# Adding the down-projection results to the residual rows by accumulating DMAs instead of on VectorE, in a decoder layer on one Trainium2 core

## The chip, the cores and the metric

The kernel runs on one core of a Trainium2 chip. The metric is the device time of one execution in microseconds (us); several runs are made, and their median is quoted. Engines are named as in the profile: PE is TensorE's matmuls, PEld its weight loads, DVE is VectorE, ACT is ScalarE, POOL is GpSimd, and SP is SyncE, which issues most DMAs. All arithmetic is on 32-bit floats.

## The reference, cut to what matters

One decoder layer over 256 rows of width 2048. The change touches the first and the last sub-layer, the two feed-forward networks (width 5632), with the DeepNorm residual around each:

```
x = layer_norm(ALPHA * x + 0.5 * (silu(x @ w_gate) * (x @ w_up)) @ w_down, ln1_g, ln1_b)
... attention sub-layer: x = layer_norm(ALPHA * x + mix, ln2_g, ln2_b) ...
x = layer_norm(ALPHA * x + 0.5 * (silu(x @ w_gate) * (x @ w_up)) @ w_down, ln3_g, ln3_b)
```

The kernel computes twice the argument of the feed-forward norms, `2*ALPHA*x + ffn(x)`, and makes up for the factor in the norm's epsilon.

## The kernel before, in words

**Rows and residual.** The 256 rows are two row tiles `t` of 128 partitions. `y[t]` (128x2048 f32, in SBUF) holds the residual rows; column block `n` is 512 wide. In the first network `y` is the input, loaded in eight pieces by `load_y` from SP's queue, one after each weight piece of the first up product. In the second network it is the normalised output of attention: `ln_res` multiplies by the gain (L591) and adds the bias (L592) on DVE, with gain and bias loaded by POOL's queue (L587, L588).

**Products.** Each f32 product is made of three matmuls of rounded halves: `split` writes `hi` on ACT (L91) and the remainder `lo` on DVE (L92), and `mm3` issues hi*hi, lo*hi and hi*lo (L96 to L98). Weights come by DMA into `raw` tiles, are split into `whi` and `wlo` tiles (six of each), and only then can PE use them.

**`gemm2`** makes a 256x1024 product (two row tiles, two column blocks) from weight pieces of 256 rows. For some pieces (`seven`) it uses seven block products for eight: DVE makes sums of weight blocks (L293 to L295), which are split as well, and the seven products gather in PSUM banks. After the last such piece ACT and DVE combine four banks into four `w` tiles (L332 to L336; `w` has nine buffers). At its end, DVE adds each remaining bank to its `w` tile (L345), and `finish` takes the four results.

**Order.** A network runs: gate 0, up 0, gate 2, up 2, gate 4, **down 0**, up 4, gate 6, up 6, gate 8, **down 1**, up 8, the last columns, down 2. The down product is so cut along its inner dimension into three groups `gi`, and each group adds its result to `y`. Groups 0 and 1 are two `gemm2` each (`cp` 0 and 1), so there are four results of 128x512 at the end of each, and 2 networks x 2 groups x 2 = 8 such ends, at about 262, 303, 513, 554, 1312, 1353, 1564 and 1605 us. In `down`, `fin` adds a result on DVE: for group 0 it also scales (`y = 2*ALPHA*y + result`, L503), for groups 1 and 2 it is a plain add (L505). After group 2 the norm follows.

**Queues.** PE and SP run in the order in which the code is written. On DVE, ACT and POOL a list scheduler sets the order at build time from its own estimates; on the chip each engine then goes strictly in that order.

Of the kernel before, what the change touches and what calls it, by code (L numbers as in the profile page):

```python
# [14 lines left out]
OP = mybir.AluOpType  # L15
# [3 lines left out]
P = 128  # L19
D = 2048  # L20
S = 256
NT = S // P
FF = 5632
KD = D // P
NCH = 512
ALPHA = 2.0 ** 0.25
# [13 lines left out]
GATE, GATE7 = (0, 1, 2, 3, 4, 5, 6, 7), (2, 4, 5)  # L40
UP, UP7 = (0, 1, 3, 2, 4, 6, 5, 7), (1, 2, 4, 5)
# [8 lines left out]
def layer(ctx: ExitStack, tc: tile.TileContext, a: dict, out: bass.AP):  # L50
    nc = tc.nc
    PE, V, A, G = nc.tensor, nc.vector, nc.scalar, nc.gpsimd
# [127 lines left out]
    def new_bank():  # L180
        return bank.tile([P, NCH], F32, name="bank")
# [166 lines left out]
    def new_T():  # L348
        return (tp.tile([P, 4, P], F32R, name="thi"), tp.tile([P, 4, P], F32R, name="tlo"))

    def sl(pair, j):
        return pair[0][:, j, :], pair[1][:, j, :]
# [5 lines left out]
    y = [const.tile([P, D], F32, name=f"y{t}") for t in range(NT)]  # L358
# [12 lines left out]
    def parts(s):  # L371
        hl = am2(F32R)
        split(*hl, s)
        return hl
# [50 lines left out]
    def ffn(name, x, xs, done, begin=None, after=None, late=()):  # L425
        wg, wu, wd = (W[name + n] + (W2[name + n][0],) for n in ("_w_gate", "_w_up", "_w_down"))
        groups = [[0, 1, 2, 3], [4, 5, 6, 7], [8, 9, 10]]
        late = list(late)
        hT, hS, hs, sg = {}, {}, {}, {}

        def trans(cs, ready, want=()):

            for c in cs:
                v, sums_too = [], c in want
                for t in range(NT):
                    while held[0] or now[0] < ready:
                        yield 1
                    pt = new_bank().rearrange("p (a b) -> p a b", a=4)
                    for j in range(4):
                        PE.transpose(pt[:, j, :], hs[c, t][:, j * P:(j + 1) * P], ident)  # L440
                    hT[c, t] = new_T()
                    src = pt
                    if sums_too:
                        src = wk([P, 4, P])
                        A.copy(src, pt)
                        v.append(src)
                    A.copy(hT[c, t][0], pt)
                    V.tensor_tensor(hT[c, t][1], src, f(hT[c, t][0]), op=OP.subtract)  # L448
                    if t and sums_too:
                        for i in range(KT):  # L450
                            hS[2 * c + i] = parts(sums([u[:, KT * i + j] for u in v for j in range(KT)]))
                    yield 1

        def gate(c0):
            def fin(t, j, r):
                A.activation(r, r, AF.Silu)
                sg[c0 + j, t] = r

            if c0:
                gemm2(x, xs, GATE, GATE7, name + "_w_gate", c0 // 2, fin)  # L460
                return
            def first(t, j, ps):
                sg[j, t] = wk([P, NCH])
                A.activation(sg[j, t], ps, AF.Silu)

            def rest(at):
                if begin and at == 7:
                    cst.update(load_consts())
                for _ in range(2):
                    if late:  # L470
                        late.pop(0)()

            gemm2(x, xs, GATE, (), name + "_w_gate", 0, first, each=rest, head=0 if begin else 4, pre=begin)

        def up(c0):
            def fin(t, j, r):
                hs[c0 + j, t] = sg[c0 + j, t]
                V.tensor_tensor(hs[c0 + j, t], r, sg[c0 + j, t], op=OP.mult)

            gemm2(x, xs, LATE if c0 in (4, 8) else UP, UP7, name + "_w_up", c0 // 2, fin, each=after if c0 == 0 else None)  # L480
            spawn(trans((c0, c0 + 1), now[0] + DFF, (0, 1, 4, 5, 9)), "T")

        def last():

            def fin(t, j, r):
                if j == 0:
                    A.activation(r, r, AF.Silu)
                    hs[10, t] = r
                else:
                    V.tensor_tensor(hs[10, t], r, hs[10, t], op=OP.mult)  # L490

            gemm2(x, xs, GATE, GATE7, name + "_gu", 0, fin)
            spawn(trans((10,), now[0] + DLAST), "T")

        def down(gi):
            grp = groups[gi]
            ks = list(range(grp[0] * 4, (grp[-1] + 1) * 4))
            xh = lambda k, t: sl(hT[k // 4, t], k % 4)

            def fin(t, n, ps):  # L500
                yc = y[t][:, n * NCH:(n + 1) * NCH]
                if gi == 0:
                    V.scalar_tensor_tensor(yc, yc, 2 * ALPHA, ps, op0=OP.mult, op1=OP.add)  # L503
                else:
                    V.tensor_tensor(yc, ps, yc, op=OP.add)  # L505
                if gi == 2:
                    done(t, n)

            for cp in range(2):
                if gi < 2 or cp == 0:  # L510
                    base = 2 * grp[0]
                    order, sevens = (DOWN, DOWN7) if gi < 2 else (range(6), (2, 3))
                    gemm2(xh, hS, [base + i for i in order], [base + i for i in sevens], name + "_w_down", cp,
                          lambda t, j, r: fin(t, 2 * cp + j, r))
                    continue
                for n in (2 * cp, 2 * cp + 1):
                    gemm(xh, wd, n, ks, lambda t, ps: fin(t, n, ps), tail=6 if n == 3 else 0)


        for step, n in ((gate, 0), (up, 0), (gate, 2), (up, 2), (gate, 4), (down, 0), (up, 4), (gate, 6), (up, 6), (gate, 8),  # L520
                        (down, 1), (up, 8)):
            step(n)
        last()
        down(2)
# [56 lines left out]
                    xs.setdefault(2 * n + j, []).extend(v[:, 2 * j + i, :] for i in range(2))  # L581
            yield 1

    def ln_res(name, n):

        g, b = wk([P, NCH]), wk([P, NCH])
        G.dma_start(g, bcast(a[name + "_g"][0, n * NCH:(n + 1) * NCH], NCH))  # L587
        G.dma_start(b, bcast(a[name + "_b"][0, n * NCH:(n + 1) * NCH], NCH))  # L588
        for t in range(NT):
            yc = y[t][:, n * NCH:(n + 1) * NCH]  # L590
            V.tensor_tensor(yc, yc, g, op=OP.mult)  # L591
            V.tensor_tensor(yc, yc, b, op=OP.add)  # L592

    def ln_out(t, eps, gb):
        mu, r = ln_rows(t, eps)
# [10 lines left out]
        load_x(max(1, 2 * i), 2 if i else 1)  # L606

    def load_y(i):
        t, n = i // 4, i % 4
        nc.sync.dma_start(y[t][:, n * NCH:(n + 1) * NCH], a["x"][t * P:(t + 1) * P, n * NCH:(n + 1) * NCH])  # L610


    w0, ps0 = wk([P, NCH]), new_bank()
# [470 lines left out]
    def sum2(i):  # L1084
        xs2[i] = parts(sums(xs2[i]))

    ffn("ffn2", lambda k, t: sl(x2[k // 4, t], k % 4), xs2, done3,
        late=[lambda i=i: sum2(i) for i in UP7] + [lambda n=n: ln_res("ln2", n) for n in range(4)])
    drain()


# [74 lines left out]
```

## Time and profile before

| | |
|---|---|
| median of 3 runs (lowest to highest) | 1767.45 us (1766.21 to 1768.01) |
| the profiled execution: its own time, and its span | 1766.0 us, 1764.3 us |
| PE busy | 1745.0 us (99%) |
| DVE busy | 1596.6 us (90%) |
| ACT busy | 997.8 us (57%) |
| POOL busy | 17.4 us (1%) |
| DMA: SP's queue, POOL's queue | 58.1% and 0.8% of 16 engines' span |
| chain that ended last, by engine | PE 74%, DVE 17%, DMA 3%, issue 3%, ACT 2% |

The own time is the device time of that one execution; the span goes from its first to its last instruction. A busy PE here is a PE with a matmul in flight; matmuls overlap, so whether PE is at its pace is read from the distance between their starts.

### The profile page before, as it was taken

To read this page: it belongs to the slowest core of one execution; us is meant where nothing else is said; L and a number is where in the kernel's file an instruction comes from. 1 tells how busy PE (TensorE), PEld (TensorE's weight loads), DVE (VectorE), ACT (ScalarE), POOL (GpSimd) and SP (SyncE) were. 2 spreads that over 40 slices of the span, in tenths; PEclk is the share of its full clock that TensorE was granted. 3 is DMA by queue.
4 is the path that set the end of the run, shared out by engine and by line. 5 is a ranking of instruction groups with operands and counts; after the bars stand their busy time and mean duration, and the time that the engine had idled before them with its cause. 6 is when DMAs were issued, how large, how long until landed. Compare 5 with 4: busy or idle time off the path is not lost.

```text
span 1764.3 us, 22385 instructions
## 1 busy us (share of the span) xinstructions
PE 1745.0 (99%) x8018; PEld 1429.0 (81%) x8018; DVE 1596.6 (90%) x2121; ACT 997.8 (57%) x1324; POOL 17.4 (1%) x40
## 2 busy tenths in 40 slices
PE   9999999999999999999999999999999999999997
PEld 7888888888888888887788778888888888888886
DVE  7899999999999998766576679899999999999997
ACT  6656555575655565654555555565655565655651
POOL 0000000000000000000000001000000000000000
PEclk9999999999999999999999999999999999999999
DMA  9665656556567557546843355656556656566654
GB/s 335 219 209 176 209 200 203 192 189 211 196 197 230 193 177 255 182 143 210 300 153 120 123 176 171 211 179 198 196 193 224 203 185 209 196 196 216 203 197 162
DMA packets 103440, 350.01 MB, mean 198 GB/s; under 512 B 11152, under 2 KB 13728, under 8 KB 103328
## 3 DMA queue, kind: packets, MB, share of 16 engines
q1 hardware_dynamic: 102016, 344.37, 58.1%
q0 software_dynamic: 1312, 4.21, 0.8%
q8 instruction: 63, 1.03, 0.2%
q14 instruction: 49, 0.40, 0.1%
HBM read 346.44 MB, written 2.10 MB: 198 GB/s over the span
## 4 chain that ended last, share of the span: by engine, by line
PE 74%; DVE 17%; DMA 3%; issue 3%; ACT 2%; SPq 0%; POOL 0%; DVEq 0%; ACTq 0%; POOLq 0%
PE bank L97 23%; PE bank L98 23%; PE bank L96 23%; DVE wlo L92 8%; DVE sum L293 2%; DVE w L345 2%; ACT whi L91 1%; DMA raw<-in_ffn_w_down 1%; DVE sum L295 1%; DVE sum L294 1%; DMA raw<-in_ffn_w_up 1%; DVE tlo L448 1%; PE bank L1004 1%; DMA raw<-in_w_in 1%; PE bank L994 1%
## 5 line engine op out<-in xcount | busy, mean ns | idle before, releaser
L96 PE MATMUL bank<-whi,thi 128*128 128x512 f32 (+1 forms) x1958 | 771.9, 394 | 0.0
L97 PE MATMUL bank<-wlo,thi 128*128 128x512 f32 (+1 forms) x1958 | 761.2, 389 | 1.5 <-DVE wlo L92 1.4
L98 PE MATMUL bank<-whi,tlo 128*128 128x512 f32 (+1 forms) x1958 | 761.1, 389 | 0.0
L91 ACT CAST whi<-raw 128x1024 fp32r<-128x1024 f32 (+2 forms) x569 | 533.1, 965 | 264.7 <-PE bank L98 123.2
L92 DVE TENSOR_TENSOR wlo<-raw,whi 128x1024 fp32r<-128x1024 f32 (+2 forms) x569 | 624.0, 1111 | 63.6 <-ACT whi L91 62.9
L91 ACT CAST whi<-sum 128x1024 fp32r<-128x1024 f32 x267 | 279.2, 1050 | 369.3 <-DVE sum L295 143.2
L96 PEld LDWEIGHTS bank<-whi,thi 128*128 128x128 f32 x1958 | 368.0, 188 | 79.1 <-issue 5.4
L98 PEld LDWEIGHTS bank<-whi,tlo 128*128 128x128 f32 x1958 | 367.6, 188 | 76.5
L97 PEld LDWEIGHTS bank<-wlo,thi 128*128 128x128 f32 x1958 | 368.2, 188 | 75.8 <-DVE wlo L92 3.8
L92 DVE TENSOR_TENSOR wlo<-sum,whi 128x1024 fp32r<-128x1024 f32 x267 | 319.3, 1214 | 26.0 <-ACT whi L91 23.7
L97 PE MATMUL bank<-wlo,m 128*128 128x512 f32 x424 | 166.0, 392 | 2.0 <-DVE wlo L92 2.0
L96 PE MATMUL bank<-whi,m 128*128 128x512 f32 x424 | 165.1, 389 | 0.0
L98 PE MATMUL bank<-whi,m 128*128 128x512 f32 x424 | 165.1, 389 | 0.0
L293 DVE TENSOR_TENSOR sum<-raw 128x1024 f32<-128x1024 f32 x106 | 129.0, 1217 | 9.1 <-DMA raw<-in_ffn_w_down 5.0
L97 PEld LDWEIGHTS bank<-wlo,m 128*128 128x128 f32 x424 | 79.5, 188 | 22.3 <-DVE wlo L92 5.5
L96 PEld LDWEIGHTS bank<-whi,m 128*128 128x128 f32 x424 | 79.6, 188 | 16.6
L98 PEld LDWEIGHTS bank<-whi,m 128*128 128x128 f32 x424 | 79.6, 188 | 16.0
L345 DVE TENSOR_TENSOR w<-bank,w 128x512 f32<-128x512 f32 x120 | 78.7, 681 | 0.2
L295 DVE TENSOR_TENSOR sum<-sum,raw 128x512 f32<-128x512 f32 x106 | 72.3, 683 | 0.2
L294 DVE TENSOR_TENSOR sum<-sum,raw 128x512 f32<-128x512 f32 x106 | 72.3, 683 | 0.0
L733 ACT ACTIVATE w<-w,mx 128x256 f32<-128x256 f32 (+1 forms) x48 | 21.4, 446 | 29.8 <-DVE mx L729 28.1
L440 PEld LDWEIGHTS bank<-ident,w 128*128 128x128 f32 x176 | 21.9, 140 | 5.8
(190 smaller groups left out, 889.7 us busy)
## 6 DMA issues: line engine op xcount, KB each, us to landing
raw<-in_ffn_w_down SPq DMA_DIRECT2D x169, 512.0 KB, 4.7
raw<-in_ffn_w_up SPq DMA_DIRECT2D x160, 512.0 KB, 4.8
raw<-in_ffn_w_gate SPq DMA_DIRECT2D x146, 512.0 KB, 5.0
raw<-in_ffn_gu SPq DMA_DIRECT2D x32, 512.0 KB, 4.2
raw<-in_w_in SPq DMA_DIRECT2D x30, 512.0 KB, 5.1
raw<-in_w_out SPq DMA_DIRECT2D x20, 512.0 KB, 3.3
sum<-in_w_in SPq DMA_DIRECT2D x18, 512.0 KB, 5.4
sum<-in_ffn_w_gate SPq DMA_DIRECT2D x12, 512.0 KB, 4.1
```

Of the source, the lines that this page charges most:

```text
L91: A.copy(hi, src)
L92: V.tensor_tensor(lo, src, f(hi), op=OP.subtract)
L96: PE.matmul(ps, xh, wh, start=first, stop=False)
L97: PE.matmul(ps, xh, wl, start=False, stop=False)
L98: PE.matmul(ps, xl, wh, start=False, stop=last)
L293: V.tensor_tensor(t13, a_, b_[:, 1:2, :].broadcast_to([P, 2, NCH]), op=OP.add)
L294: V.tensor_tensor(t24[:, 0], t13[:, 0], a_[:, 1], op=OP.add)
L295: V.tensor_tensor(t24[:, 1], t24[:, 0], b_[:, 0], op=OP.add)
L345: V.tensor_tensor(rest[b], B[b], rest[b], op=OP.add)
L440: PE.transpose(pt[:, j, :], hs[c, t][:, j * P:(j + 1) * P], ident)
L448: V.tensor_tensor(hT[c, t][1], src, f(hT[c, t][0]), op=OP.subtract)
L733: A.activation(s[:, h, :], s[:, h, :], AF.Exp, bias=mx[:, h:h + 1], accum_out=sm[:, h:h + 1])
```

## The change

For groups 0 and 1 the four results of each `gemm2` are no longer added by DVE but by DMAs issued from POOL's queue that add their source to the destination in SBUF. As such a DMA only adds, `y` is multiplied by `2*ALPHA` beforehand, on ACT: in the first network two weight pieces after the load of each piece of `y` (the last two during gate 2), in the second network at the end of `ln_res`. Group 2 is left as it was.

```
-                gemm2(x, xs, GATE, GATE7, name + "_w_gate", c0 // 2, fin)
+                gemm2(x, xs, GATE, GATE7, name + "_w_gate", c0 // 2, fin,
+                      each=(lambda i: after(8 + i)) if after and c0 == 2 else None)
...
             def fin(t, n, ps):
                 yc = y[t][:, n * NCH:(n + 1) * NCH]
-                if gi == 0:
-                    V.scalar_tensor_tensor(yc, yc, 2 * ALPHA, ps, op0=OP.mult, op1=OP.add)
+                if gi < 2:
+                    G.dma_start(yc, ps, accum_op=OP.add)
                 else:
                     V.tensor_tensor(yc, ps, yc, op=OP.add)
-                if gi == 2:
                     done(t, n)
...
+    def scale_y(t, n):
+        yc = y[t][:, n * NCH:(n + 1) * NCH]
+        A.mul(yc, yc, 2 * ALPHA)
+
-    def ln_res(name, n):
+    def ln_res(name, n, scale=False):
...
             V.tensor_tensor(yc, yc, b, op=OP.add)
+            if scale:
+                scale_y(t, n)
...
     def load_y(i):
-        t, n = i // 4, i % 4
-        nc.sync.dma_start(y[t][:, n * NCH:(n + 1) * NCH], a["x"][t * P:(t + 1) * P, n * NCH:(n + 1) * NCH])
+
+        if i < 4 * NT:
+            t, n = i // 4, i % 4
+            nc.sync.dma_start(y[t][:, n * NCH:(n + 1) * NCH], a["x"][t * P:(t + 1) * P, n * NCH:(n + 1) * NCH])
+        if 0 <= i - 2 < 4 * NT:
+            scale_y((i - 2) // 4, (i - 2) % 4)
...
-        late=[lambda i=i: sum2(i) for i in UP7] + [lambda n=n: ln_res("ln2", n) for n in range(4)])
+        late=[lambda i=i: sum2(i) for i in UP7] + [lambda n=n: ln_res("ln2", n, True) for n in range(4)])
```

DVE's instructions at the end of the first network's first down `gemm2` (about 262 us; `y_92` and `y_93` are `y` of the two row tiles), before:

```order
L294 TENSOR_TENSOR sum<-sum,raw 128x512
L92 TENSOR_TENSOR wlo<-raw,whi 128x512
L345 TENSOR_TENSOR w<-bank,w 128x512 x2
L503 SCALAR_TENSOR_TENSOR y_92<-y_92,w 128x512
L345 TENSOR_TENSOR w<-bank,w 128x512
L503 SCALAR_TENSOR_TENSOR y_93<-y_93,w 128x512
L503 SCALAR_TENSOR_TENSOR y_92<-y_92,w 128x512
L345 TENSOR_TENSOR w<-bank,w 128x512
L295 TENSOR_TENSOR sum<-sum,raw 128x512
L503 SCALAR_TENSOR_TENSOR y_93<-y_93,w 128x512
L92 TENSOR_TENSOR wlo<-sum,whi 128x1024 x2
```

The same place in the change:

```order
L294 TENSOR_TENSOR sum<-sum,raw 128x512
L92 TENSOR_TENSOR wlo<-raw,whi 128x512
L345 TENSOR_TENSOR w<-bank,w 128x512 x4
L295 TENSOR_TENSOR sum<-sum,raw 128x512
L92 TENSOR_TENSOR wlo<-sum,whi 128x1024
```

The four L503 are gone, and the block sum L295 with the splits behind it moves up by that much. The other seven ends read alike (L505 for L503 in group 1).

ACT's instructions near the end of the first network's first up product (75 to 84 us), before:

```order
L91 CAST whi<-sum 128x1024 x2
L91 CAST whi<-raw 128x1024 x2
L332 COPY w<-bank 128x512
L91 CAST whi<-raw 128x1024 x5
L91 CAST whi<-raw 128x512
```

The same place in the change (L586 is `scale_y`):

```order
L91 CAST whi<-sum 128x1024
L586 ACTIVATE y_93<-y_93 128x512
L91 CAST whi<-sum 128x1024
L91 CAST whi<-raw 128x1024 x2
L332 COPY w<-bank 128x512
L91 CAST whi<-raw 128x1024 x5
```

The scaling of the last piece of `y` now stands between two weight splits; the first seven stand in the same manner ahead of it, one or more splits apart. POOL's queue gets 16 adding DMAs in a row per network, and nothing stands between them.

## Rows read from the trace of the kernel before

**Rows 1.** Windows: busy us of PE, PEld, DVE, ACT, POOL; clock, DMA share, GB/s.

```profile
300.00:350.00 50.00, 50.00 (x222) 41.40 (x221) 49.32 (x60) 25.83 (x29) 0.00 (x0) 1.00 0.59 199
...
1550.00:1600.00 50.00, 49.42 (x217) 40.18 (x216) 48.61 (x57) 27.05 (x30) 0.00 (x0) 1.00 0.63 205
```

**Rows 2.** Timeline of PE: start us, us, engine, line, operation, near 300 us.

```profile
299.69 0.39 PE L96 MATMUL bank<-whi,thi 128*128 128x512 f32 x1
...
301.96 0.39 PE L97 MATMUL bank<-wlo,thi 128*128 128x512 f32 x1
```

**Rows 3.** Waits of PE over the span, longest first: us in total, times, longest.

```profile
PE bank L97 <- DVE wlo L92: 3.4, 9, 0.7
```

**Rows 4.** Timeline of PE at four waits: in brackets idle and releaser.

```profile
393.42 0.39 PE L96 MATMUL bank<-whi,thi 128*128 128x512 f32 x1
394.28 0.50 PE L97 MATMUL bank<-wlo,thi 128*128 128x512 f32 x1 [0.47 <-DVE wlo L92]
...
394.85 0.40 PE L96 MATMUL bank<-whi,m 128*128 128x512 f32 x1
395.42 0.50 PE L97 MATMUL bank<-wlo,m 128*128 128x512 f32 x1 [0.17 <-DVE wlo L92]
...
1323.44 0.39 PE L96 MATMUL bank<-whi,m 128*128 128x512 f32 x1
1324.09 0.50 PE L97 MATMUL bank<-wlo,m 128*128 128x512 f32 x1 [0.26 <-DVE wlo L92]
...
1575.21 0.40 PE L96 MATMUL bank<-whi,m 128*128 128x512 f32 x1
1576.19 0.50 PE L97 MATMUL bank<-wlo,m 128*128 128x512 f32 x1 [0.58 <-DVE wlo L92]
```

**Rows 5.** Chain by line: 292 to 396, 1290 to 1326, 1540 to 1577 us.

```profile
by line: DVE wlo L92 33.9%; issue 13.1%; DMA raw<-in_ffn_w_up 10.0%; DVE sum L293 8.9%; DVE w L345 5.9%; DVE sum L295 4.7%; DVE sum L294 4.7%; ACT whi L91 4.0%; DVE m L92 2.0%; DVE y L503 1.9%; DVE w L478 1.9%; DVE tlo L448 1.7%; DVE w L333
...
by line: DVE wlo L92 36.6%; DMA raw<-in_ffn_w_down 17.7%; DVE sum L293 9.9%; issue 9.3%; DVE y L503 6.7%; DVE w L345 6.7%; DVE sum L294 5.0%; DVE sum L295 5.0%; PE bank L97 2.7%; PE bank L98 1.9%; PE bank L96 1.3%; DVEq L293 0.1%
...
by line: DVE wlo L92 38.7%; DMA raw<-in_ffn_w_down 18.9%; DVE sum L293 9.5%; DVE sum L295 6.7%; DVE w L345 6.5%; DVE y L505 6.5%; issue 6.5%; DVE sum L294 4.9%; PE bank L97 1.3%; PE bank L96 0.6%; PE bank L98 0.6%; DVEq L293 0.1%
```

**Rows 6.** Groups by form: line, engine, operation, shapes, xcount; busy us, mean ns; idle before.

```profile
L505 DVE TENSOR_TENSOR y<-w,y 128x512 f32<-128x512 f32 x24 | 16.0, 678 | 0.0
...
L503 DVE SCALAR_TENSOR_TENSOR y<-y,w 128x512 f32<-128x512 f32 x16 | 10.6, 682 | 0.0
```

**Rows 7.** Groups by form: the nearest ACT instruction, 128x512 from SBUF to SBUF.

```profile
L456 ACT ACTIVATE w<-w 128x512 f32<-128x512 f32 x32 | 19.4, 633 | 7.0 <-DVE w L345 7.0
```

**Rows 8.** The last load of `y` (SP's queue), and ACT's split at 78 us.

```profile
L610 SPq DMA_DIRECT2D y<-in_x x1: 421/421/421, 73.5 to 73.5; - x1
...
DMA to landing us min/median/max: 4.9/4.9/4.9
...
78.44 1.05 ACT L91 CAST whi<-sum 128x1024 fp32r<-128x1024 f32 x1 [1.89 <-DVE sum L295]
```

**Rows 9.** Window of 1072 to 1090 us, and its DMAs by queue and tile.

```profile
1072.00:1090.00 18.00, 18.00 (x81) 14.92 (x80) 17.99 (x31) 10.85 (x12) 4.32 (x8) 1.00 0.76 264
...
q0 software_dynamic: 640, 2.10, 39.0%
...
raw<-in_ffn_w_up SPq DMA_DIRECT2D x5, 512.0 KB, 6.2
```

**Rows 10.** Page, DMA issues: engine, xcount, KB each, median us to landing.

```profile
raw<-in_ffn_w_up SPq DMA_DIRECT2D x160, 512.0 KB, 4.8
```

**Rows 11.** Timeline of DVE: first add of a result, next reuse of `w`.

```profile
261.97 0.68 DVE L503 SCALAR_TENSOR_TENSOR y<-y,w 128x512 f32<-128x512 f32 x1
...
292.18 0.68 DVE L333 TENSOR_TENSOR w<-bank,w 128x512 f32<-128x512 f32 x1
```

**Rows 12.** Windows behind two ends of down products: columns as in the first group.

```profile
1311.00:1316.00 5.00, 5.00 (x24) 4.14 (x23) 5.00 (x10) 0.00 (x0) 0.00 (x0) 1.00 0.33 108
1316.00:1321.00 5.00, 5.00 (x24) 4.14 (x23) 5.00 (x5) 3.46 (x4) 0.00 (x0) 1.00 0.31 105
```

## The prediction

> **What bounds the kernel now.** I read the windows first, then the timeline of PE, PE's waits, and the chain behind the larger waits. In the feed-forward stretches PE and DVE are full at once: from 300 to 350 us PE is busy 50.00 of 50 us with 222 matmuls, DVE 49.32 [rows 1]. Which of the two sets the pace is read from PE's starts. Near 300 us there are 11 starts from 299.69 to 301.96 us, that is 0.227 us each [rows 2], and 222 matmuls of that length fill 50 us. So PE runs at its own pace there, and a DVE that gets freer does not make it faster. DVE counts only where PE stands still for it. Those places are few: PE waits for the low half of a weight (`wlo`) nine times, 3.4 us in all [rows 3]. From 1550 to 1600 us one sees it: 217 matmuls instead of 222, with DVE at 48.61 [rows 1]. The 17% that DVE holds of the chain of the whole kernel is therefore no measure of the gain; most of it is work that PE's own pace hides, and the reader is to keep the 3.4 us in mind as the size of what can be had.
>
> Four of the nine waits have an add of a down result in the chain behind them. At 1323 us PE's starts are 0.65 us apart where 0.227 is normal, at 1575 us 0.98, at 393 us 0.86 and at 395 us 0.57 [rows 4]. Over the normal distance that is 0.42 + 0.75 + 0.63 + 0.34 = 2.14 us. The chain into the first two is DVE work nearly throughout, and the adds hold 6.7% of 36 us and 6.5% of 37 us of it, 2.4 us each, which are the four adds of one end; in the chain into 393 us L503 holds 1.9% of 104 us, 2.0 us [rows 5]. Each share is larger than the wait at its end.
>
> **What is removed.** 32 adds on DVE: 16 of 0.682 us and 16 of the 24 rows of 0.678 us [rows 6], 21.8 us of DVE, 2.7 us at each of the eight ends of a down `gemm2`. DVE's order shows that the block sum L295 and the splits behind it move up by the four adds. Taken out of the chain, 2.0 to 2.4 us are more than the 0.42, 0.75 and 0.63 + 0.34 us that PE waits, so these four waits should go: 2.14 us. What is late next is PE itself, which then goes on at 0.227 us. At the other ends PE does not wait, so 2.7 us less of DVE buys nothing there; up products and the attention have none of the removed rows. The other five of the nine waits I leave as they are: I found no add in the stretches behind them.
>
> **What is added on ACT.** 16 scalings of 128x512. The trace has no such multiply; the nearest row is an activation of that size from SBUF to SBUF, 0.633 us [rows 7]. That is 10.1 us, hidden by an ACT that is busy 26 to 27 of 50 us [rows 1]. Without that cover it would cost up to 0.63 us each. The order can make it dearer, since ACT goes strictly in turn: a scaling whose piece of `y` has not landed holds up the weight splits behind it, and these hold up DVE and then PE. The worst is the last one. Its load is issued at 73.5 us and lands 4.9 us later, at 78.4; ACT stands idle for 1.89 us up to 78.44, waiting for DVE, just where the order puts the scaling [rows 8]. So the scaling waits for 1.8 us that are idle anyway, and the split behind it starts 0.6 us late. A delay of 0.6 us is a third of the one gap shown, and ACT is idle for nearly half of its time, so I put all 16 at 0; the bound above is eight pieces at 0.6 us, 5 us, if nothing hid them. In the second network the scalings wait for DVE's L592, which comes at its time as before, and stand between splits in the same manner.
>
> **What is added as DMAs.** 32 adds of 256 KB, issued by POOL, which is otherwise idle. The trace has no adding DMA and none within SBUF. The nearest are POOL's loads of the norm's gain and bias, also 128x512. Eight of them fall in 1072 to 1090 us and take 39.0% of 18 us of all 16 DMA engines [rows 9], 0.88 us each. Four adds at that price are 3.5 us per end. I take that as the lower bound, since an add must also read what it adds to.
>
> The Trainium skill has the price of that second read: in "Collectives: The Full Stack" (The bandwidth ceiling) the add itself is free, but two sources are read for each write on one ring, and the measured rate is about half. By it an add would be an estimated 1.8 us and an end 7 us, and the sum would stay, since that is no more than the eight loads took together.
>
> Whether it matters is a question of how late the weights come. The eight loads are a fair rehearsal, 7.0 us of DMA in one burst: the five weight loads in that window land in 6.2 us [rows 9] against 4.8 [rows 10], 1.4 us later, and PE loses nothing (81 matmuls in 18 us, busy 18.00). And the adds come at a good moment: after an end the DMA share is 0.33 and 0.31 for ten microseconds [rows 12], because the raw buffers are held by DVE work. A delay of 1.4 us is less than the 2.4 us by which DVE is now earlier. I take 0, and carry what is left to the second rival.
>
> The adds bring one new wait: a `w` tile may be written again only when its DMA is done. After the first end the next writers are ACT's L332 and DVE's L333; DVE's comes 30 us after the first add [rows 11], ACT's a little before it. So four adds may take some 7 us each before L332 waits, with the weight splits behind it on ACT and PE behind those. Behind an add on POOL stand only other adds until the norm. Group 2 reads `y` only after two more whole products, up 8 and the last columns.
>
> **The sum.** From the profiled execution's 1766.0 us: less 2.14 for the four waits, 0 for ACT, 0 for the DMAs, makes 1763.9. That execution lies 1.45 us under the median of the runs shown, 1767.45, so the median is forecast at 1765.3, 0.12% less. A difference under 0.2%, 3.5 us, I call no change: it is about what a measurement of this kernel can tell.
>
> **The rivals.** *Every wait for DVE goes.* If the earlier DVE carries over into the other five waits too, or they go with a shifted order, the gain is at most all 3.4 us of idleness. Four waits with 1.48 us of idleness cost 2.14 us, 1.45 times as much, so 4.9 us, and the time is 1762.5. For it: DVE is near 50 of 50 us for long stretches, so time saved can travel far. Against it: none of the five has a removed add in the stretch behind it.
>
> *The stalls stay.* DVE may spend what it saves waiting for the high halves, which ACT can only write once PE frees a buffer; then the lead is the same when the next heavy stretch comes, and the changed order can put another sum or split late. Then the time is 1767.4. For it speaks that DVE's order also changed where nothing was removed; against it that the chains into 1323 and 1575 us run without a break of PE through the removed adds.
>
> *The adds crowd out the weights.* If an add is much dearer than a load, the weights behind an end come late. Seven microseconds of loads made them 1.4 us late, so four adds at four times the price of a load, 14 us, make them 2.8 us late; the relief at the two ends that wait now is 2.4 less 0.4, 2.0 us. That leaves 0.8 us at each of eight ends, 6.4 us: 1773.9. It is slower by 0.2%, 3.5 us, from 0.44 us per end on, which is 2.44 us late; at 1.4 us for 7.0 us of DMA that is 12.2 us for four adds, 3 us per add. The row for it is that there is none of an adding DMA; against it the low DMA share after the ends. The Trainium skill's rule stands beside it: by "DMA: Bandwidth & Descriptors" (Issuing engines are not separate DMA queues), DMAs of all issuers run on the same 16 engines and interleave; the trace agrees, in that the weights were later beside POOL's loads.
>
> **How the numbers follow.** Forecast 0.52, stalls stay 0.22, every wait goes 0.11, weights crowded 0.15. The first two are within 0.2%, the third faster, the fourth slower: same 0.74, faster 0.11, slower 0.15. The forecast's own range is 1762.5 (the third case) to 1767.4 (the second). The range of 8 in 10 reaches from 1762.4 halfway into the crowded case, 1771.5.
>
> **What would show it.** Right: PE's waits for `wlo` near 2 us instead of 3.4, none at the first heavy stretch after a down end in the second network; DVE busy 22 us less, ACT 10 us more; PE's starts 0.227 us apart as before; weight loads after an end landing within 2 us of their time. Wrong: adding DMAs that take over 3 us each or land more than 25 us after their issue; ACT waiting for a DMA at L332; waits of ACT at L586 longer than its idleness there; new waits of PE behind the ends.

## The result, and the profile after

The changed kernel takes 1781.62 us (median of six runs, 1775.66 to 1781.91) where the kernel before takes 1766.58 on the same chip (six runs, 1764.96 to 1768.01). The ratio is 1.0081, interval 1.0070 to 1.0092: slower by 0.8%. The forecast was 1765.3 us, and the range ended at 1771.5.

The page of the changed kernel, busy time of four engines, then POOL's DMA queue (packets, MB, share of 16 engines' span):

```profile
PE 1749.0 (98%) x8018; PEld 1428.0 (80%) x8018; DVE 1577.5 (89%) x2089; ACT 1006.8 (57%) x1340; POOL 45.4 (3%) x72
...
q0 software_dynamic: 5920, 12.60, 3.7%
```

The removed and added work has about the size that the prediction gave it: DVE is 19.1 us less busy, ACT 9.0 us more. What an add costs the DMA engines follows from the queue: 3.7% of 1779.6 us less the 0.8% of 1764.3 us of the kernel before is 51.7 us for 32 adds, 1.62 us each, nearly twice the 0.88 us of a load of that size [rows 9].

Waits over the span, first of PE for `wlo`, then of DVE for the loads of `w_up` (us in total, times, longest):

```profile
PE bank L97 <- DVE wlo L92: 11.6, 15, 1.7
```

```profile
DVE sum L293 <- DMA raw<-in_ffn_w_up: 37.1, 19, 6.1
```

PE waits for `wlo` 11.6 us instead of 3.4 [rows 3]. The second row is the new thing: L293, the first sum of weight blocks of a `seven` piece, waits for its load. In the kernel before the same row reads 4.0 us, 3 times, longest 2.4. Where that hits PE is seen in windows (columns as in [rows 1]):

```profile
300.00:350.00 50.00, 47.10 (x204) 37.51 (x203) 41.57 (x47) 24.72 (x27) 3.45 (x4) 1.00 0.66 199
550.00:600.00 50.00, 48.53 (x212) 39.34 (x211) 41.45 (x46) 25.43 (x27) 3.50 (x4) 1.00 0.67 209
1300.00:1350.00 50.00, 50.00 (x222) 41.43 (x221) 49.56 (x55) 31.17 (x35) 3.52 (x4) 1.00 0.75 230
1360.00:1410.00 50.00, 48.26 (x210) 38.92 (x209) 42.75 (x50) 24.65 (x27) 3.49 (x4) 1.00 0.67 206
1550.00:1600.00 50.00, 50.00 (x222) 41.42 (x221) 49.92 (x57) 28.43 (x32) 3.48 (x4) 1.00 0.77 232
1600.00:1650.00 50.00, 49.59 (x220) 40.73 (x219) 42.58 (x48) 26.16 (x28) 3.51 (x4) 1.00 0.68 212
```

The same in the kernel before, where [rows 1] does not have it (550, 1360 and 1600 us):

```profile
550.00:600.00 50.00, 50.00 (x223) 41.39 (x222) 49.90 (x60) 26.16 (x28) 0.00 (x0) 1.00 0.61 204
1360.00:1410.00 50.00, 50.00 (x222) 41.42 (x221) 49.94 (x57) 28.98 (x31) 0.00 (x0) 1.00 0.61 204
1600.00:1650.00 50.00, 50.00 (x222) 41.39 (x222) 49.91 (x60) 26.53 (x29) 0.00 (x0) 1.00 0.64 210
```

Read the matmul counts. Around 1575 us, where the first end of a product lies, PE now does 222 matmuls where it did 217 [rows 1]: the stall that the change was forecast to remove there is gone. From 300 to 350 us, behind a second end (`cp` 1), it does 204 where it did 222, and DVE, full before, is at 41.57 us. The same holds behind the second ends of 561 and 1364 us, with 212 and 210 matmuls where the kernel before did 223 and 222. Behind the last second end, at 1618 us, only 2 of 222 are missing. These four windows lack 43 matmuls, 9.7 us at PE's pitch of 0.2265 us. Over the whole span, counting every distance between starts that is more than 0.05 us over the pitch, PE loses 48.9 us, before 34.0: 14.9 us more, of the 15.3 us by which the span grew. What does not lie in the four windows comes later: at the start of up 6, where PE loses some 2 us each near 399 and 1457 us (before 1.0 and 0.6), and near 648 and 1705 us, where it waits for DVE's L345.

One such place in DVE's timeline (idle before, and releaser, in brackets), then PE's:

```profile
303.50 2.48 DVE L345 TENSOR_TENSOR w<-bank,w 128x512 f32<-128x512 f32 x4
305.89 0.68 DVE L295 TENSOR_TENSOR sum<-sum,raw 128x512 f32<-128x512 f32 x1
306.49 1.82 DVE L92 TENSOR_TENSOR wlo<-raw,whi 128x1024 fp32r<-128x1024 f32 x2
308.23 1.22 DVE L92 TENSOR_TENSOR wlo<-sum,whi 128x1024 fp32r<-128x1024 f32 x1
315.50 1.23 DVE L293 TENSOR_TENSOR sum<-raw 128x1024 f32<-128x1024 f32 x1 [6.05 <-DMA raw<-in_ffn_w_up]
316.64 1.22 DVE L92 TENSOR_TENSOR wlo<-sum,whi 128x1024 fp32r<-128x1024 f32 x1
```

```profile
316.65 0.39 PE L96 MATMUL bank<-whi,m 128*128 128x512 f32 x1
317.91 0.50 PE L97 MATMUL bank<-wlo,m 128*128 128x512 f32 x1 [0.88 <-DVE wlo L92]
```

DVE stands for 6.05 us at L293, although the split behind it, `wlo<-sum`, belongs to an earlier piece. PE then waits for just that split, and twice more for `wlo` by 331 us. DVE's waits at the other three second ends are 4.83, 4.96 and 4.98 us. They are not by themselves PE's losses: behind the last of them PE still does 220 of 222 matmuls. Two things have to be known about such a row: why the load is late, and why DVE stands there at all.

The load: windows of 304 to 314 us, first of the kernel before, then of the changed one; then the first two of SP's `w_up` loads issued behind that end (ns to issue, first and last issue) and their time from issue to landing, in the same order:

```profile
304.00:314.00 10.00, 10.00 (x46) 8.29 (x45) 10.00 (x14) 3.62 (x5) 0.00 (x0) 1.00 0.49 172
```

```profile
304.00:314.00 10.00, 10.00 (x46) 8.29 (x45) 5.44 (x8) 3.67 (x4) 3.45 (x4) 1.00 1.01 226
```

```profile
L289 SPq DMA_DIRECT2D raw<-in_ffn_w_up x2: 327/478/628, 309.9 to 311.1; - x2
DMA to landing us min/median/max: 3.6/4.2/4.8
```

```profile
L289 SPq DMA_DIRECT2D raw<-in_ffn_w_up x2: 327/754/1181, 307.7 to 308.3; - x2
DMA to landing us min/median/max: 7.7/8.0/8.3
```

The four adds start at 304.5 us, the two loads are issued at 307.7 and 308.3, and the DMA engines are full. The loads take some 4 us longer from issue to landing than before. As they are also issued 2.2 and 2.8 us earlier, they land 1.9 and 0.7 us later: at 315.4 and 316.6 us where it was 313.5 and 315.9. The Trainium skill, "DMA: Bandwidth & Descriptors" (Issuing engines are not separate DMA queues), has the transfers of all issuers on the same 16 engines; the rows agree.

DVE, on the other side, comes to the sum at 309.45 us, 5.0 us earlier than in the kernel before, where the sum ran without a wait:

```profile
314.43 1.22 DVE L293 TENSOR_TENSOR sum<-raw 128x1024 f32<-128x1024 f32 x1
```

The additions taken off account for 2.7 us of the 5.0; the rest is two splits that now stand behind the sum. So DVE's 6.05 us have two sides: a load that lands later, and a DVE that is there earlier. The order: DVE's rows at this place as the list scheduler set them, first of the kernel before, then of the changed one (the number is the place in DVE's list, equal neighbours counted once):

```
293 L293 TENSOR_TENSOR sum<-raw 128x1024
294 L503 SCALAR_TENSOR_TENSOR y_93<-y_93,w 128x512
295 L294 TENSOR_TENSOR sum<-sum,raw 128x512
296 L92 TENSOR_TENSOR wlo<-raw,whi 128x1024
297 L295 TENSOR_TENSOR sum<-sum,raw 128x512
298 L92 TENSOR_TENSOR wlo<-raw,whi 128x512
299 L92 TENSOR_TENSOR wlo<-sum,whi 128x1024 x2
300 L92 TENSOR_TENSOR wlo<-raw,whi 128x1024
301 L293 TENSOR_TENSOR sum<-raw 128x1024
```

```
287 L295 TENSOR_TENSOR sum<-sum,raw 128x512
288 L92 TENSOR_TENSOR wlo<-raw,whi 128x1024
289 L92 TENSOR_TENSOR wlo<-raw,whi 128x512
290 L92 TENSOR_TENSOR wlo<-sum,whi 128x1024
291 L293 TENSOR_TENSOR sum<-raw 128x1024
292 L92 TENSOR_TENSOR wlo<-sum,whi 128x1024
293 L294 TENSOR_TENSOR sum<-sum,raw 128x512
294 L295 TENSOR_TENSOR sum<-sum,raw 128x512
295 L92 TENSOR_TENSOR wlo<-raw,whi 128x1024 x3
```

With four rows less on DVE, the scheduler has drawn the second L293 (the fifth piece of up 4) forward, ahead of one split of the third piece's sums (row 292) and of both splits of the fourth piece (in row 295), of which one stood ahead of it before. The text ahead of the prediction says that the other ends read like the first one; the four second ends do not.

### The profile page after: what moved, and what is told of

The parts are those of the page before. It is cut to its first block, busy times and chain, and to the rows that moved or that the text cites. A ratio compares the mean times of both kernels' runs of the same rounds, so it can differ in the third digit from the quotient of the medians.

```text
span 1779.6 us, 22478 instructions
## 1 busy us (share of the span) xinstructions
PE 1749.0 (98%) x8018; PEld 1428.0 (80%) x8018; DVE 1577.5 (89%) x2089; ACT 1006.8 (57%) x1340; POOL 45.4 (3%) x72
## 4 chain that ended last, share of the span: by engine, by line
PE 45%; DVE 36%; DMA 9%; issue 7%; ACT 2%; SPq 0%; DVEq 0%; POOL 0%; ACTq 0%; POOLq 0%
DVE wlo L92 18%; PE bank L97 14%; PE bank L98 14%; PE bank L96 14%; DMA raw<-in_ffn_w_up 5%; DVE sum L293 5%; DVE w L345 3%; DMA raw<-in_ffn_w_down 3%; DVE sum L294 2%; DVE sum L295 2%; ACT whi L91 1%; DVE tlo L448 1%; DVE w L479 1%; PE bank L1014 1%; DVE w L333 1%
## 5 line engine op out<-in xcount | busy, mean ns | idle before, releaser
L293 DVE TENSOR_TENSOR sum<-raw 128x1024 f32<-128x1024 f32 x106 | 129.1, 1218 | 40.2 <-DMA raw<-in_ffn_w_up 37.1
L345 DVE TENSOR_TENSOR w<-bank,w 128x512 f32<-128x512 f32 x120 | 77.0, 679 | 0.0
L295 DVE TENSOR_TENSOR sum<-sum,raw 128x512 f32<-128x512 f32 x106 | 72.3, 682 | 0.2
L294 DVE TENSOR_TENSOR sum<-sum,raw 128x512 f32<-128x512 f32 x106 | 72.3, 682 | 0.0
L504 POOL DMA_DIRECT2D y<-w x32 | 27.9, 1227 | 1062.6 <-DVE w L345 1024.7
```

What stands on the lines that cost most here:

```text
L293: V.tensor_tensor(t13, a_, b_[:, 1:2, :].broadcast_to([P, 2, NCH]), op=OP.add)
L294: V.tensor_tensor(t24[:, 0], t13[:, 0], a_[:, 1], op=OP.add)
L295: V.tensor_tensor(t24[:, 1], t24[:, 0], b_[:, 0], op=OP.add)
L345: V.tensor_tensor(rest[b], B[b], rest[b], op=OP.add)
L504: G.dma_start(yc, ps, accum_op=OP.add)
```

## The experiments

Three theories. **Crowding**: the adds make the weight loads late, and that alone costs the time. **Order**: a DVE that goes strictly in turn and has a load drawn forward loses the time, whatever the DMAs do. **Both**: the load must be late and the sum in front of ready work. All runs in one table; each ratio is to the kernel before on the same chip:

| Run | DVE's order in up 4, up 8 | adding DMAs | median us | ratio (interval) |
|---|---|---|---|---|
| changed kernel | changed | 32 | 1781.62 | 1.0081 (1.0070 to 1.0092) |
| e1_no_adds | changed | none | 1768.33 | 1.0004 (0.9994 to 1.0013) |
| e7_traffic | of before | 32 | 1769.71 | 1.0014 (1.0005 to 1.0023) |
| e9_double_traffic | of before | 64 | 1773.64 | 1.0035 (1.0021 to 1.0049) |
| e4_copy | changed | 32 plain copies | 1769.93 | 1.0018 (1.0008 to 1.0028) |
| e3_second_ends | its own, near the changed | 16, second ends | 1779.59 | 1.0077 (1.0062 to 1.0092) |
| e2_first_ends | its own, near the changed | 16, first ends | 1768.82 | 1.0006 (0.9994 to 1.0017) |
| e5_order | sums held back | 32 | 1769.61 | 1.0011 (1.0001 to 1.0021) |
| e5b_one_row | one sum held back | 32 | 1767.33 | 1.0001 (0.9992 to 1.0010) |
| e10_first_ends_order | sums held back | 16, first ends | 1769.81 | 1.0014 (1.0005 to 1.0024) |
| e6_scale_only | of before | none | 1766.35 | 0.9991 (0.9982 to 1.0000) |
| e11_later_sums | one sum held back, others later | 32 | 1764.06 | 0.9980 (0.9971 to 0.9988) |
| e12_later_sums_before | others later | none | 1769.09 | 1.0009 (1.0000 to 1.0018) |

### Order without DMAs, DMAs without order

e1_no_adds: the changed kernel, less the additions.

```
             def fin(t, n, ps):
                 yc = y[t][:, n * NCH:(n + 1) * NCH]
-                if gi < 2:
-                    G.dma_start(yc, ps, accum_op=OP.add)
-                else:
+                if gi == 2:
                     V.tensor_tensor(yc, ps, yc, op=OP.add)
                     done(t, n)
```

> The changed kernel without the first two down products' additions to the residual rows (left out altogether, so those products are missing from the output); ACT's scalings stay, and VectorE's order is that of the changed kernel row for row, L293 drawn ahead of ready splits included. Order alone (a VectorE that stands on a load drawn forward): the loss stays, 1778 to 1781 us. Crowding alone (adding DMAs delay the weight loads behind a second end): the loss goes, 1764 to 1766 us, and the w_up loads at 308 us land in 3.6 to 4.8 us again. Both needed together: 1765 to 1767 us, with VectorE still seen waiting at L293 but by under 3 us instead of 5 to 6 us.

1768.33 us: the order alone costs nothing that can be measured, so that theory is out by itself. Crowding alone was to give 1764 to 1766 and both together 1765 to 1767; the time is a little over either. DVE still stands at the drawn-forward L293, but for 2.05 us, because the loads land in time again. DVE's timeline of e1_no_adds, and the landing of the loads of 303 to 316 us:

```profile
313.97 1.23 DVE L293 TENSOR_TENSOR sum<-raw 128x1024 f32<-128x1024 f32 x1 [2.05 <-DMA raw<-in_ffn_w_up]
```

```profile
DMA to landing us min/median/max: 3.5/3.7/5.6
```

e7_traffic: the kernel before, with the DMA behind DVE's own addition.

```
                     V.tensor_tensor(yc, ps, yc, op=OP.add)
+                if gi < 2:
+                    G.dma_start(yc, ps, accum_op=OP.add)
                 if gi == 2:
                     done(t, n)
```

> The kernel before with VectorE's additions kept and, behind each of the first two products' additions, the same adding DMA of the changed kernel (so these products count twice in the output). VectorE's order is that of the kernel before, its work too; the DMA traffic is that of the changed kernel. Crowding alone: 1778 to 1783 us. Order alone: 1766 to 1768 us. Both needed together: 1766 to 1770 us, with w_up loads behind the second ends landing in over 6 us but few new PE waits.

1769.71 us, in the range of both together; crowding alone is out. The loads are late here too, but no sum has been drawn forward, and DVE waits little: at the place of the 6.05 us it waits 1.3. The landing of the loads from 303 to 316 us, DVE's waits over the span, and a window of 1449 to 1452 us:

```profile
DMA to landing us min/median/max: 4.8/5.8/6.0
```

```profile
DVE sum L293 <- DMA raw<-in_ffn_w_up: 9.7, 9, 3.0
```

```profile
1448.80:1452.20 3.40, 3.40 (x10) 2.66 (x9) 3.40 (x4) 0.00 (x0) 0.00 (x0) 0.51 0.43 152
```

The adds follow DVE's own additions one by one here, and the loads take only 1.6 us longer than before, not 4, so this run alone does not show what loads as late as the changed kernel's would do; e5b_one_row below does. What PE loses more than before lies mostly at 1445 to 1452 us, the start of up 6, with no adding DMA near: a wait of 1.45 us for `wlo`, then a granted clock of 0.51.

The order alone adds 0.04%, the DMAs alone 0.14%, and both 0.81%: 0.63%, some 11 us, exists only where the two meet.

### How much traffic

e4_copy: the order of the changed kernel row for row, with plain copies.

```
-                    G.dma_start(yc, ps, accum_op=OP.add)
+                    G.dma_start(yc, ps)
```

> The changed kernel with every adding DMA turned into a plain copy of the same 256 KB between the same tiles (so the residual rows are overwritten, not added to); the order on every engine is that of the changed kernel row for row. If the time that an adding DMA takes of the 16 engines sets how late the loads land (a copy should take about half, 0.8 to 1.0 us against 1.6 us): the w_up loads at 308 us land in 5 to 6.5 us, VectorE stands 3 to 4 us at L293, and the time lies between, 1769 to 1776 us. If it is the number of DMAs or their issue on POOL: 1778 to 1782 us as in the changed kernel.

1769.93 us, between, and near the end without traffic. The other case, that the number of DMAs or their issue on POOL costs the time, is out. The loads at 307 us were expected to land in 5 to 6.5 us and DVE to stand 3 to 4 us; they land in 3.5 and 4.7 us, and DVE stands 1.9 us there. e9_double_traffic is e7_traffic with the DMA's line written twice.

```
                 if gi < 2:
                     G.dma_start(yc, ps, accum_op=OP.add)
+                    G.dma_start(yc, ps, accum_op=OP.add)
```

> The kernel before with VectorE's additions kept and two adding DMAs of 256 KB behind each of the first two products' additions instead of one (these products count three times in the output); VectorE's order is that of before. If late loads cost nothing as long as no sum is drawn forward onto them: 1767 to 1771 us, as with one. If there is a point from which crowding alone decides, as the rival of the prediction had it from about 3 us per product tile: 1773 to 1790 us, with VectorE's waits for w_up at the second ends over 3 us.

1773.64 us, at the lower edge of the second case: with 64 adds, crowding alone does cost 0.35%. But not as expected: DVE's longest wait for `w_up` behind a second end is 1.6 us, not over 3, and PE does all its matmuls there (300 to 350 us). It loses most behind first ends, with 81 and 121 matmuls in the other two windows, where the kernel before does 90 and 129:

```profile
300.00:350.00 50.00, 50.00 (x223) 41.39 (x222) 48.39 (x59) 25.71 (x29) 6.90 (x8) 1.00 0.81 246
1325.00:1345.00 20.00, 19.31 (x81) 14.70 (x81) 19.04 (x22) 11.63 (x15) 2.60 (x4) 1.00 0.93 256
1575.00:1605.00 30.00, 28.69 (x121) 22.02 (x121) 28.59 (x31) 17.94 (x21) 4.20 (x5) 1.00 0.88 240
```

POOL's queue in e4_copy, then in e9_double_traffic:

```profile
q0 software_dynamic: 3872, 12.60, 2.1%
```

```profile
q0 software_dynamic: 10528, 20.99, 6.3%
```

A copy takes (2.1% of 1768.8 less 14.1) / 32 = 0.72 us of the 16 engines, an add in e9_double_traffic (6.3% of 1771.7 less 14.1) / 64 = 1.52 us. So the loss is not proportional to the traffic: with the order changed, 0.72 us per tile costs 3 us of time, and 1.62 us costs 15.

### Which ends

e3_second_ends and e2_first_ends: DMAs at one kind of end, DVE's additions at the other (e2_first_ends has `n < 2`).

```
-                if gi < 2:
+                if gi < 2 and n >= 2:
                     G.dma_start(yc, ps, accum_op=OP.add)
                 else:
                     V.tensor_tensor(yc, ps, yc, op=OP.add)
-                    done(t, n)
+                    if gi == 2:
+                        done(t, n)
```

> The changed kernel with adding DMAs only at each product's second end (16 of 32); at the first ends VectorE adds. If the loss comes from late w_up loads behind the second ends met by a VectorE that has drawn L293 forward there (late loads and order together): most of it is there, 1776 to 1782 us, with 5 to 6 us of VectorE standing at L293 near 310, 570, 1370 and 1630 us. If every adding DMA costs its share of the shared transfers wherever it stands: half of it, 1772 to 1775 us.

> The changed kernel with adding DMAs only at each product's first end (16 of 32); at the second ends VectorE adds. The second ends then have no adding DMA beside the w_up loads, and VectorE's second L293 stands two splits further back. Crowding alone (only second ends hurt): 1765 to 1767 us; crowding at every end would leave half, 1772 to 1775 us. Order alone: 1766 to 1771 us. Both needed together: 1765 to 1767 us.

1779.59 and 1768.82 us: the kernel with 16 adds at second ends keeps nearly the whole loss, the one with 16 at first ends nothing that can be told from zero. In the changed kernel DVE waits for nothing from 262 to 300 us, behind the first of the first ends, although the DMA share is high there too (0.80). So in these kernels the cost does not belong to an add as such; it belongs to what stands behind it.

Both runs have orders of their own, so they say less about the one row. In both, the fifth piece's sum stands behind both splits of the third piece's sums, and of earlier work only the fourth piece's splits stand behind it. In e3_second_ends DVE waits 3.4 to 4.3 us there, not the 5 to 6 expected, and part of PE's loss lies behind first ends, where DVE still adds: 214 matmuls from 250 to 300 us, before 222.

### One row held back

e5_order lets no sum of up 4 and up 8 stand ahead of the split written before it; e5b_one_row does so for the fifth piece alone. `behind` gives the scheduler a dependence of one DVE instruction on another, and DMAs, PE and SP stay as they are.

```
+    def behind(i, j):
+        tc.add_manual_dep(i.ins, j.ins.name, mybir.DependencyInfo(mybir.DependencyClass.NoSync, mybir.DependencyReason.DATA), reason="order")
...
-                split(hi[:, :n], lw[:, :n], v[:, :n])
+                keep.append(split(hi[:, :n], lw[:, :n], v[:, :n]))
...
-                V.tensor_tensor(t13, a_, b_[:, 1:2, :].broadcast_to([P, 2, NCH]), op=OP.add)
+                s = V.tensor_tensor(t13, a_, b_[:, 1:2, :].broadcast_to([P, 2, NCH]), op=OP.add)
+                if kps is LATE and at == 4:
+                    behind(s, keep[-1])
```

In e5_order the condition is `kps is LATE and len(keep) >= 4`.

> The changed kernel with one addition: in up 4 and up 8 a sum of two weight tiles (L293) may not stand ahead of the split written before it on VectorE, so that no ready split stands behind a load that has not landed. All adding DMAs stay. Crowding alone: 1777 to 1782 us. Order alone: 1763 to 1766 us, slightly faster than the kernel before. Both needed together: 1764 to 1768 us.

> The changed kernel with one sum held back in each of up 4 and up 8: the L293 of the fifth piece, which the changed kernel drew ahead of ready splits onto the late load, may not stand ahead of the split written before it; the other sums are left to the scheduler. Late loads and order together: 1765 to 1770 us, as with all sums held back. If other rows drawn forward matter as much: 1771 to 1777 us.

1769.61 us, 1.6 over the range given for both together, and 1767.33 us, within its own. With all 32 adds and one sum per up product held back, the whole loss is gone. Beside the changed kernel's timeline, that of e5b_one_row at the same place (L296 is L293 here, and L299 is L294), then the landing of the loads issued from 303 to 309 us, and two windows behind second ends:

```profile
308.07 2.35 DVE L92 TENSOR_TENSOR wlo<-sum,whi 128x1024 fp32r<-128x1024 f32 x2
311.61 1.23 DVE L92 TENSOR_TENSOR wlo<-raw,whi 128x1024 fp32r<-128x1024 f32 x1 [1.19 <-ACT whi L91]
314.32 1.22 DVE L92 TENSOR_TENSOR wlo<-raw,whi 128x1024 fp32r<-128x1024 f32 x1 [1.49 <-ACT whi L91]
315.47 1.22 DVE L296 TENSOR_TENSOR sum<-raw 128x1024 f32<-128x1024 f32 x1
```

```profile
DMA to landing us min/median/max: 3.4/7.4/8.1
```

```profile
300.00:350.00 50.00, 50.00 (x223) 41.40 (x222) 46.86 (x55) 24.69 (x28) 3.46 (x4) 1.00 0.66 201
1360.00:1410.00 50.00, 50.00 (x222) 41.41 (x221) 46.82 (x54) 27.10 (x30) 0.88 (x2) 1.00 0.65 206
```

The two loads are as late (7.4 and 8.1 us against 7.7 and 8.3), and the sum starts at the same time, 315.47 against 315.50 us. But three splits are done by then that stood behind it in the changed kernel, and PE does all its matmuls. The late load itself costs nothing here; what stood behind it did. (The two orders of DVE are the same up to the held sum. Behind it the scheduler also sorts other rows anew, in up 4 and later, so the kernels differ in more than this row, and the share of the one row is not shown by itself.)

e10_first_ends_order has e2_first_ends' DMAs and e5_order's held sums.

> Adding DMAs at the first ends only, VectorE's additions at the second ends, and the sums of up 4 and up 8 held behind the splits written before them. Late loads and order together: nothing is late and nothing drawn forward, so the kernel comes out with that of before or a little under it, 1764 to 1767.5 us. If the work taken off VectorE were worth anything by itself it would show here as under 1764 us; if the rest of the loss is the adding DMAs anywhere: 1768 to 1769 us.

1769.81 us: the expectation missed, and over every case that it named. Its PE loses most at 1443 us, as e5_order's does at 1442, at the start of up 6 in the second network, where no adding DMA is near. Windows of e5_order there:

```profile
1430.00:1442.00 12.00, 12.00 (x59) 9.94 (x58) 10.98 (x29) 8.98 (x17) 0.00 (x0) 1.00 0.26 98
1442.00:1445.10 3.10, 0.43 (x2) 0.01 (x1) 3.10 (x6) 2.93 (x5) 0.00 (x0) 0.90 0.00 0
1445.10:1451.20 6.10, 6.03 (x14) 4.77 (x15) 6.10 (x7) 2.92 (x4) 0.00 (x0) 0.50 0.70 220
```

and PE's timeline:

```profile
1445.17 0.80 PE L100 MATMUL bank<-wlo,thi 128*128 128x512 f32 x1 [2.74 <-DVE wlo L92]
```

The wait is for `wlo`, which stands behind the operand sums of up 4's transposed rows on a full DVE, and after it PE's granted clock is 0.50 for 6 us. With no add near, this speaks for the new order; but e7_traffic loses there in the order of before, so what sets this loss is not shown.

### The scalings, and a version that beats both

e6_scale_only is the changed kernel with DVE's addition for all three groups.

```
-                if gi < 2:
+                if False:
                     G.dma_start(yc, ps, accum_op=OP.add)
                 else:
                     V.tensor_tensor(yc, ps, yc, op=OP.add)
-                    done(t, n)
+                    if gi == 2:
+                        done(t, n)
```

> The scalings alone: ACT scales the rows as in the changed kernel, but VectorE does all additions (a plain add where the kernel before had a scaled one), and there is no adding DMA. If the scalings are free, as the prediction had it: 1765.5 to 1768.5 us, the time of before. If they take ACT's splits' place: 1769 us or more, with PE waits for whi near 60 to 80 us and 1060 to 1130 us.

1766.35 us: the scalings on ACT cost nothing that can be measured, as forecast.

e5b_one_row keeps stalls of 2.0 and 1.8 us at 392 and 1445 us, where `wlo` of up 6 stands on DVE behind the operand sums of up 4's transposed rows. e11_later_sums adds to it that these sums, and some of PE's transposes behind them, are written later, the sums by two steps; e12_later_sums_before has that alone, in the kernel before.

```
                     if t and sums_too:
+                        if c in (4, 5):
+                            yield 1
+                            yield 1
                         for i in range(KT):
```

> The one-row version (the fifth piece's sum held back, all adding DMAs) with the operand sums of up 4's transposed rows written two steps later, so that they no longer stand ahead of up 6's first splits on VectorE. The stalls of PE that the one-row version keeps at 392 and 1445 us (2.0 and 1.8 us) should go; if so 1763 to 1765 us, faster than both kernels. If something else on VectorE is late there: 1766 to 1769 us.

> The kernel before with only the operand sums of up 4's transposed rows written two steps later. Its stalls at 393 to 395 us (0.97 us beyond the pitch) go and those of 1443 to 1445 us (0.7 us): 1764.5 to 1767 us. Beside the version with adding DMAs it shows whether taking the additions off VectorE is worth anything: if that comes out over 1 us lower, yes.

e11_later_sums takes 1764.06 us, faster than the kernel before by 0.2% and, going by the two ratios, than the changed one by 1%. PE's waits, and two of its windows:

```profile
PE bank L100 <- DVE wlo L92: 1.9, 6, 0.6
```

```profile
300.00:350.00 50.00, 50.00 (x222) 41.40 (x222) 46.64 (x55) 24.69 (x28) 3.45 (x4) 1.00 0.65 200
...
1550.00:1600.00 50.00, 50.00 (x222) 41.41 (x221) 49.63 (x56) 28.82 (x31) 3.48 (x4) 1.00 0.79 248
```

e12_later_sums_before, expected at 1764.5 to 1767, takes 1769.09 us and missed: PE's waits at 393 to 396 us are gone, but new ones of 1.0 us in all stand at 523 to 527 us. In the kernel before, the later sums alone do not help. Between the two versions, on the same chip, lie 5.0 us, made up of the 32 additions taken off DVE, the held sum, and the orders that the scheduler made of each. Whether any of it is the change's own is not shown: no run has the held sum without the adding DMAs.

## Why the prediction was wrong, point by point

**PE runs at its own pace: right.** e11_later_sums has the 222 matmuls per 50 us that the prediction counted, and the changed kernel's new losses outside the attention are waits of PE for DVE.

**The four waits go, 2.14 us: half of it.** The windows around the first ends of the second network show 222 matmuls each in the changed kernel. Those at the start of up 6 stayed (in e5b_one_row one of 2.0 us): other rows of DVE, the operand sums, are late there. They went only when those were moved.

**ACT's scalings at 0: right**, by e6_scale_only.

**The price of an add: the lower bound was taken for the argument, and it was too low.** 0.88 us was put down as the bound, 1.62 us was measured, against 0.72 us for a plain copy. The estimate of 1.8 us worked out from the Trainium skill, "Collectives: The Full Stack" (The bandwidth ceiling), was nearer: the page has it for the reduce step of a collective, which reads two sources for each write and runs at about half the rate of a copy. The runs here show more than that, 2.25 times a copy. That the estimate came so close is partly luck: it doubled the 0.88 us of a load, and twice the copy measured within SBUF would be 1.44 us.

**The adding DMAs at 0: the step that failed.** The prediction said that the loads would be 1.4 us late, as beside POOL's loads at 1072 us, and that this was less than the 2.4 us by which DVE would be early. Each half fails. The loads behind a second end take some 4 us longer (8.0 against 4.2): the low DMA share of 0.33 and 0.31 [rows 12] was read behind a first end, for both of these windows lie behind the one at 1312 us, while from 304 to 314 us it was 0.49 before any add was there. And the comparison of one lateness with one earliness takes it that DVE does the same rows in the same order. It does not: DVE comes to the sum 5.0 us earlier, not 2.4, with ready splits left behind it, and there an earlier DVE only waits longer, 6.05 us. The prediction itself said that DVE's order also changed where nothing was removed, and priced that at no more than the stalls staying. Late loads with the order of before cost 2.4 us (e7_traffic), the new order with loads in time 1 us (e1_no_adds), and both together 15.

**The rival of crowded weights: its direction, not its mechanism.** It was given 0.15 and 1773.9 us, with every end paying in proportion, and a threshold of 3 us per add. At 1.6 us per add it should not have decided, and alone it does not. Twice the traffic in the order of before, 3.0 us per result, costs 0.35%, where the rival had 0.2%; so that threshold was of the right size, but the cost lies behind the first ends and not at every end in proportion. Of the prediction's signs of being wrong, one came: new waits of PE behind the ends. What the rivals lacked is the pair: a late load and a row drawn forward in front of ready work.

## What to carry to other kernels

Taking work off an engine whose order a scheduler sets makes a new order for that engine; look in it for every row that needs a DMA and has moved ahead of rows that don't, and read from the trace when that DMA lands. Here a late load cost nothing while only its own user waited (e5b_one_row); it cost time when an engine that goes strictly in turn had the load's first user in front of ready work. An engine that comes to such a row earlier gains nothing by it: it waits there for as much longer. Where such a row is found, one dependence that holds it back may be worth more than the change itself.

## What the runs showed of the hardware

An adding DMA of 128x512 within SBUF takes 1.62 us of all 16 DMA engines, a plain copy 0.72 us; the median from issue to landing is 6.5 us for the add and 3.0 us for the copy.

After a wait of 2.74 us PE's granted clock was 0.50, its lower level of 1.2 GHz, for about 6 us (the windows of e5_order above): 14 matmuls there lie some 0.43 us apart in place of 0.227, 2.8 us more on top of the wait. It does not follow every such wait: in e5b_one_row the clock was 0.50 for 3.3 us after a wait of 1.86 us at 392 us, and 1.00 after one of 1.63 us at 1445 us. Nor does the longer wait decide: in e7_traffic the clock was 0.51 after one of 1.45 us (its window above). The windows of e5b_one_row behind its two waits:

```profile
394.60:397.90 3.30, 3.30 (x9) 2.56 (x8) 3.30 (x4) 1.38 (x2) 0.00 (x0) 0.50 0.77 256
...
1447.20:1452.00 4.80, 4.80 (x21) 4.00 (x22) 4.80 (x5) 1.68 (x2) 0.00 (x0) 1.00 0.68 218
```

In the changed kernel no wait for `wlo` was over 1.7 us, and the clock stayed at 1.00 in the windows around its second ends. What decides between the two levels is open.
